# Making the second half's matmul operands in four parts instead of six, in the later half of a block

## The chip, the cores and the metric

The kernel runs on one core of one Trainium2 chip. The metric is the device time of one execution in microseconds (us). Several engines work side by side on a core, each with its own queue of instructions in a fixed order: PE (TensorE, the matmuls), DVE (VectorE), ACT (ScalarE), POOL (GpSimd) and SP (SyncE, which here issues nearly all transfers). An instruction waits at the head of its queue until what it needs is there, and everything behind it in that queue waits with it.

## The reference

One encoder layer over 2048 tokens of width 1024, all in fp32. Cut to the places that matter here:

```
h = rms_norm(x, norm1_g);  proj = h @ w_in                    # 1024 x 3584
dq, dk, dv, rq, rk, rv, rg = split(proj)                      # seven blocks of 512 columns
a = diff_attention(rms_norm(dq), rms_norm(dk), dv)            # 4 heads, softmax
y = retention(rq, rk, rv) in both directions, gated by rg
x1 = x + concat(a, y) @ w_out
out = x1 + gelu_mlp(rms_norm(x1, norm2_g), w_mlp1, w_mlp2)    # 1024 x 4096 x 1024
```

## The kernel before

Every fp32 operand of a large product is split into a high and a low part (`hi`, `lo`, rounded to fp32r), and a product is three matmuls: high by high, high by low, low by high (lines 36 to 38). `split_sbuf` makes the high part on ACT (line 44) and the low part on DVE (line 50).

The products with w_in and w_mlp1 go in halves of 1024 tokens (g = 0 and g = 1) and in blocks of 512 columns, and each block is one Strassen-Winograd step (`winograd_block`): seven products of half-size matrices instead of eight. The token side of the seven products are the *units*, in the order of PE: b11, b21, t2, t1, t3, b22, t4 (`UNITS`), where t1 to t4 are differences of the quarter matrices b11, b12, b21, b22. The weight side are a11, a12, the sums s2, s1, s3, s4 (made by POOL on line 277) and a22; each is split into `wh` and `wl` two products ahead of its use. The raw weights of a block come in two transfers into tiles r0 and r1 (line 687). They share the tag "raw", with three buffers, with a third tile, x2, so a new x2 can be loaded only when the last reader of the x2 before is done.

The units of the first half are made before its products start. Those of the second half are made beside the first half's products, 128 tokens of each quarter at a time, by the generator `fill_parts`, in blocks 1 to 4 of the w_in stage (rk, rv, rg and q; the seven blocks go rq, rk, rv, rg, q, k, v) and in blocks 1 to 4 of the stage of w_mlp1. For a fill, SP loads x2 (256 tokens; lines 875 and 1489). In the w_in stage the tokens are then normed: ACT sums the squares (L775), DVE and ACT make the root (L68 to L73), DVE scales x2 (L880). Then PE transposes 16 tiles of 128x128 into PSUM (L180, tile `htp`), DVE multiplies them by the gain back into x2 (L183), DVE and POOL make the differences t1 to t4 in place (L146; t1 and t2 on DVE, t3 and t4 on POOL), ACT and DVE split each unit, and SP stores the parts to DRAM (L253: `b11hd`, `b11ld` and so on), from where the second half loads them.

`winograd_block` calls `between(unit)` each time the instructions of a product have been written, and that call draws the next part from the generator; after the block a loop draws what is left. The code is not a fixed schedule: a list scheduler reorders the instructions of each engine by its own estimate, so the place of a part in the code bounds where its instructions go but does not fix it.

In the q block each finished result is also normed per head (L710 and L711 for the squares and their sum, L68 to L73 the root, L715 the scaling), transposed on PE (L752, tile `pq`) and split (L59). In the rg block POOL gates the results (L733, L734).

Of the kernel before, what the change touches and what calls it, by code (L numbers as in the profile page):

```python
# [40 lines left out]
def split_sbuf(nc, hi, lo, src, eng_hi, eng_lo):  # L41

    if eng_hi == "act":
        nc.scalar.activation(hi, src, AF.Copy)  # L44
    elif eng_hi == "pool":
        nc.gpsimd.tensor_scalar(hi, src, 1.0, 1.0, op0=ALU.mult, op1=ALU.mult)
    else:
        nc.vector.tensor_copy(hi, src)
    e = nc.gpsimd if eng_lo == "pool" else nc.vector
    e.tensor_tensor(out=lo, in0=src, in1=hi.bitcast(F32), op=ALU.subtract)  # L50
# [36 lines left out]
UNITS = ("b11", "b21", "t2", "t1", "t3", "b22", "t4")  # L87
# [47 lines left out]
def fill_parts(nc, pp, x2, turn, sink):  # L135


    b = {f"b{kh + 1}{th + 1}": x2[:, th, kh * H : (kh + 1) * H] for kh in range(2) for th in range(2)}

    def bring(kh):  # L140
        for th in range(2):
            ps = pp.tile([P, H], F32, tag="p", name="htp")
            turn(ps, kh, th)(b[f"b{kh + 1}{th + 1}"])

    def sub(n, x0, x1, o, eng):
        eng.tensor_tensor(out=b[o], in0=b[x0], in1=b[x1], op=ALU.subtract)  # L146
        b[n] = b[o]

    def split(n):
        hi, lo, then = sink(n)  # L150
        split_sbuf(nc, hi, lo, b[n].rearrange("p (a b) -> p a b", a=4), "act", "dve")
        then()

    bring(0)
    split("b11")
    yield
    bring(1)
    sub("t1", "b12", "b11", "b11", nc.vector)
    split("b21")
    yield  # L160
    sub("t3", "b22", "b12", "b12", nc.gpsimd)
    split("b22")
    split("t1")
    yield
    sub("t2", "b22", "t1", "b22", nc.vector)
    split("t3")
    yield
    sub("t4", "t2", "b21", "b21", nc.gpsimd)
    split("t2")
    yield  # L170
    split("t4")


# [14 lines left out]
class FirstUnits:  # L188
# [7 lines left out]
    def turn(self, kp, kh, th):  # L196
        k = kh * 4 + kp
        ps = self.pp.tile([P, H], F32, tag="p", name="htp")
        for j in range(4):
            self.nc.tensor.transpose(ps[:, j * P : (j + 1) * P], self.xs[th * 4 + j][:, k * P : (k + 1) * P], self.ident[:])  # L200
        self.turned[kp, kh, th] = ps

    def bring(self, kp, kh, th):
        k = kh * 4 + kp
        if (kh, th) == (0, 1):
            t = self.pool2.tile([P, H], F32, tag="hi", name="usrc")
        else:
            t = self.pool.tile([P, H], F32, tag="c", name="usrc", bufs=BUFS["c"])
        ps = self.turned.pop((kp, kh, th))
        self.nc.scalar.activation(t[:], ps[:], AF.Copy, scale=self.gain[:, k : k + 1])  # L210
        self.b[kp][f"b{kh + 1}{th + 1}"] = t[:]

    def split(self, kp, n, hi, lo="dve"):
        split_sbuf(self.nc, *(t[:, kp] for t in self.tb[n]), self.b[kp][n], hi, lo)

    def sub(self, kp, n, x0, x1, o, eng):
        b = self.b[kp]
        eng.tensor_tensor(out=o, in0=b[x0], in1=b[x1], op=ALU.subtract)
        b[n] = o
# [131 lines left out]
class Units:  # L351
# [13 lines left out]
    def next(self, shape, dt, name):  # L365
        self.n += 1
        return self.shared.tile(shape, dt, tag=f"p{(self.n - 1) % 6}", name=name, bufs=1)
# [196 lines left out]
def pool(tc, name, bufs, space=None, side=None):  # L564
    kw = {} if space is None else dict(space=space)
    return tc.tile_pool(name=name, bufs=bufs, side=side, reuse_waits="tile", **kw)
# [3 lines left out]
def encoder(ctx: ExitStack, tc: tile.TileContext, a: dict, out: bass.AP, dbg=None):  # L570
    nc = tc.nc
# [10 lines left out]
    def const(shape, name, dt=F32, pool=cp):  # L582
        return pool.tile(shape, dt, tag=name, name=name)
# [41 lines left out]
    t0, t1, t2 = (const([P, 24], f"lgt{i}") for i in range(3))  # L625
# [64 lines left out]
    def load_w(pool, w, c0):  # L690

        return [r for fh in range(2) for r in load_half(pool, w, c0 + fh * 256)]
# [5 lines left out]
    pp = mixer.enter_context(pool(tc, "ps_1", 8, PSUM))  # L698
    ret = Retention(nc, hp, pp, ident, wk, dict(rk=rk_d, rv=rv_d, rq=rq_d))
    with ExitStack() as ph:  # L700
        wp = ph.enter_context(pool(tc, "wst", 3))
# [94 lines left out]
        tb = winograd_units(nc, hp)  # L796
# [116 lines left out]
        for g in range(S // G):  # L913
            if g:
                first = load_w(wp, w_in, blocks[0][1] * 512)
                tb = winograd_units(nc, hp, saved[0])
            for bi, (what, blk) in enumerate(blocks):
                raws = first if bi == 0 else load_w(wp, w_in, blk * 512)
                if g == 0 and 0 < bi < 5:
                    x2 = second_load(bi - 1)  # L920
                fill = iter(())
                if g == 0 and 0 < bi < 5:
                    fill = fill_parts(
                        nc, pp, x2, turn_pair(nc, (x2[:, 0], x2[:, 1]), g1, ident), into_dram(nc, tp, "hi", saved[0], bi - 1)
                    )

                def between(unit):
                    if g and what == "v":
                        lead_in(unit)
                    if unit != "b11":  # L930
                        next(fill, None)

                winograd_block(nc, wp, pp, raws, tb, what not in ("rq", "rk"), consumer(what, g), later, between,
                    ahead, parts() if g == 0 and bi == 0 else iter(()),
                    dict(s1=s1[:], s2=s2[:]) if g == 0 and bi == 0 else {})
                ahead = {}
                if g == 0 and bi == 0:
                    small_ones()
                for _ in fill:
                    pass  # L940
# [478 lines left out]
    wp = mlp.enter_context(pool(tc, "m1w", 3))  # L1419
    pp = mlp.enter_context(pool(tc, "ps_m1", 8, PSUM))  # L1420

    def load_w1(blk):
        return [r for fh in range(2) for r in load_half(ep, w1, fh * (DFF // 2) + blk * 256)]

    with ExitStack() as ph:
        hp = ph.enter_context(pool(tc, "h2T", 1))
        for g in range(S // G):
# [4 lines left out]
            tb = tb0 | winograd_units(nc, hp, saved[1 + g], UNITS[2:], loads, ("t4", "b22", "t3", "t2", "t1"))  # L1432
            for blk in range(DFF // 512):
# [13 lines left out]
                if blk == 0:  # L1447
                    raws = first
                elif blk == 1:
                    with tc.issue_after(loads[-1].ins):  # L1450
                        raws = load_w1(blk)
                else:
                    raws = load_w1(blk)
# [30 lines left out]
                fill = iter(())  # L1484
                if g == 0 and 0 < blk < 5:
                    x2 = ep.tile([P, 2, DM], F32, tag="raw", name="x2")
                    for i in range(2):
                        r0 = (7 + 4 * i + blk) * P
                        nc.sync.dma_start(x2[:, i], x1n_d[r0 : r0 + P, :])
                    fill = fill_parts(  # L1490
                        nc, pp, x2, turn_pair(nc, (x2[:, 0], x2[:, 1]), g2, ident), into_dram(nc, wp, "d", saved[2], blk - 1)
                    )
                winograd_block(
                    nc, wp, pp, raws, tb, False, consume, [[], []], lambda unit: unit != "b11" and next(fill, None),
                    ahead=ahead, sums=sums, ptag="d",
                )
                ahead = {}
# [144 lines left out]
```

## Time and profile before

| | |
|---|---|
| median of 3 runs | 2854.14 us (2851.39 to 2856.62) |
| profiled execution | 2851.18 us, of which the span 2849.4 us |
| PE busy | 2723.1 us, 96% of the span |
| DVE, POOL, ACT busy | 1917.1, 1346.1 and 1298.5 us |
| stage of w_in, first half | up to about 330 us in the span |
| stage of w_out | 1365 to 1591 us |
| blocks 1 to 4 of w_mlp1, first half | about 1630 to 1800 us |

The span runs from the first to the last instruction that the profiler recorded; 1.8 us of the profiled execution lie around it. PE is the engine that sets the end: it is idle for 126 us of the span (2849.4 less 2723.1), and what counts for the time is where it waits and where its matmuls run at less than the full clock. "Granted clock" is the share of TensorE's full clock that the profile shows for a stretch.

### The profile page before, as it was taken

How to read it: one execution, taken by the hardware profiler on the slowest of the kernel's cores; microseconds unless marked ns; L12 is line 12 of the kernel's file. 1: busy time of each engine (PE TensorE's matmuls, PEld its weight loads, DVE VectorE, ACT ScalarE, POOL GpSimd, SP SyncE). 2: the span in 40 equal slices, each digit the busy share in tenths (PEclk: the TensorE clock that was granted, in tenths of full speed). 3: DMA queues.
4: the chain of work that ended last, by engine and by line, in shares of the span. 5: the costliest groups of instructions: out<-in, count | busy, mean ns of one | idle time of the engine just before them, and what ended most of it. 6: DMA issues, size and time to landing. Idle time of an engine off the chain costs nothing. (4 is left out here: it accounts for less than half of the span.)

```text
span 2849.4 us, 41027 instructions
## 1 busy us (share of the span) xinstructions
PE 2723.1 (96%) x15488; PEld 2333.2 (82%) x15488; DVE 1917.1 (67%) x2877; ACT 1298.5 (46%) x1842; POOL 1346.1 (47%) x778
## 2 busy tenths in 40 slices
PE   5997999998889999999899989999999999999999
PEld 4797989997778888888777777788888888888887
DVE  7888864787788999989887466555655544435432
ACT  5433422344367777777433345444445432222221
POOL 6345222513368777887443355665655103323320
PEclk8998999998899999999999999999999999999999
DMA  3564683269442313121477766767444848755461
GB/s 126 182 205 143 237 283 112 89 194 262 108 107 59 90 52 94 53 87 45 155 238 242 284 199 221 226 237 276 160 159 149 316 156 291 284 200 177 155 243 45
DMA packets 361029, 494.50 MB, mean 174 GB/s; under 512 B 23168, under 2 KB 257152, under 8 KB 352640
## 3 DMA queue, kind: packets, MB, share of 16 engines
q1 hardware_dynamic: 338608, 466.71, 49.9%
q10 hardware_dynamic: 21648, 20.98, 2.2%
q0 software_dynamic: 576, 4.19, 0.4%
q8 instruction: 122, 2.00, 0.3%
q14 instruction: 75, 0.61, 0.1%
HBM read 315.64 MB, written 176.16 MB: 173 GB/s over the span
## 5 line engine op out<-in xcount | busy, mean ns | idle before, releaser
L37 PE MATMUL p<-wl,ah 128*128 128x512 f32 x896 | 348.6, 389 | 0.0
L36 PE MATMUL p<-wh,ah 128*128 128x512 f32 x896 | 348.4, 389 | 0.0
L277 POOL TENSOR_TENSOR s<-raw 128x1024 f32<-128x1024 f32 x58 | 146.2, 2521 | 356.7 <-DMA raw<-in_w_mlp 103.7
L318 DVE TENSOR_TENSOR c<-ps,c 128x512 f32<-128x512 f32 x360 | 237.8, 684 | 114.2 <-PE ps L38 112.3
L1055 POOL TENSOR_TENSOR p<-p 128x1024 f32<-128x1024 f32 x127 | 303.3, 2412 | 0.1
L44 ACT ACTIVATE ah<-ra 128x1024 fp32r<-128x1024 f32 x112 | 112.6, 1052 | 412.5 <-PE p L37 410.8
L50 DVE TENSOR_TENSOR wl<-s,wh 128x1024 fp32r<-128x1024 f32 x120 | 192.1, 1602 | 148.8 <-ACT wh L44 148.7
L1039 ACT ACTIVATE p<-p,nm 128x2048 f32<-128x2048 f32 x128 | 256.8, 2006 | 35.7 <-DVE nm L1027 34.7
L50 DVE TENSOR_TENSOR ah<-ra,ah 128x1024 fp32r<-128x1024 f32 x76 | 103.4, 1396 | 221.4 <-ACT ah L44 221.4
L1465 POOL TENSOR_TENSOR c<-c 128x512 f32<-128x512 f32 x128 | 195.9, 1554 | 105.2 <-ACT c L1468 103.5
L44 ACT ACTIVATE wh<-s 128x1024 fp32r<-128x1024 f32 x120 | 126.5, 1056 | 245.4 <-PE ps L37 104.0
L38 PE MATMUL p<-wh,ah 128*128 128x512 f32 x608 | 236.5, 389 | 0.0
L1526 POOL TENSOR_TENSOR t<-br 128x1024 f32<-128x1024 f32 x32 | 77.7, 2429 | 335.7 <-DMA br<-in_w_mlp 176.4
L1022 PE MATMUL sc<-ka,qa 128*128 128x512 f32 x512 | 207.5, 405 | 4.1 <-DVE nm L1027 3.9
L1054 POOL TENSOR_SCALAR p<-p,ratio 128x1024 f32<-128x1024 f32 x127 | 141.9, 1130 | 144.0 <-DVE ratio L1049 110.8
L1023 PE MATMUL sc<-ka,qb 128*128 128x512 f32 x512 | 202.9, 396 | 0.0
L37 PEld LDWEIGHTS p<-wl,ah 128*128 128x128 f32 x896 | 168.2, 188 | 34.9
L36 PEld LDWEIGHTS p<-wh,ah 128*128 128x128 f32 x896 | 168.2, 188 | 34.9
L55 ACT ACTIVATE aTh<-pa 128x512 fp32r<-128x512 f32 x256 | 151.1, 591 | 83.4 <-PE pa L1216 82.0
L1027 DVE CUSTOM_DVE_ANT_0 p<-sc,bias,nm 128x1024 f32<-128x1024 f32 (+1 forms) x136 | 167.7, 1233 | 22.6 <-PE sc L1023 20.8
L1216 PEld LDWEIGHTS pa<-ident,p 128*128 128x128 f32 x1024 | 120.7, 141 | 64.1 <-issue 30.2
L56 DVE TENSOR_TENSOR aTl<-pa,aTh 128x512 fp32r<-128x512 f32 x256 | 170.3, 686 | 4.0 <-DMA vh<-vhd 3.3
(377 smaller groups left out, 8169.1 us busy)
## 6 DMA issues: line engine op xcount, KB each, us to landing
br<-in_w_mlp SPq DMA_DIRECT2D x88, 512.0 KB, 5.5
raw<-in_w_mlp SPq DMA_DIRECT2D x32, 1024.0 KB, 5.9
raw<-in_w_in SPq DMA_DIRECT2D x28, 1024.0 KB, 5.7
xt<-in_x SPq DMA_DIRECT2D x20, 512.0 KB, 5.5
q<-rqd SPq DMA_DIRECT2D x16, 512.0 KB, 10.2
qa<-qhd SPq DMA_DIRECT2D x64, 128.0 KB, 3.0
qb<-qld SPq DMA_DIRECT2D x64, 128.0 KB, 3.0
ua11d<-c SPq DMA_DIRECT2D x32, 256.0 KB, 2.2
```

The costliest lines, as they stand in the source:

```text
L36: nc.tensor.matmul(out, ah, bh, start=first, stop=False)
L37: nc.tensor.matmul(out, ah, bl, start=False, stop=False)
L38: nc.tensor.matmul(out, al, bh, start=False, stop=last)
L44: nc.scalar.activation(hi, src, AF.Copy)
L50: e.tensor_tensor(out=lo, in0=src, in1=hi.bitcast(F32), op=ALU.subtract)
L56: nc.vector.tensor_tensor(out=lo, in0=src, in1=hi.bitcast(F32), op=ALU.subtract)
L318: nc.vector.tensor_tensor(out=o[:], in0=x0[:], in1=x1[:], op=op)
L1022: nc.tensor.matmul(sc[:, o : o + 512], qa[:, c, ql], r, start=True, stop=False)
L1023: nc.tensor.matmul(sc[:, o : o + 512], qb[:, c, ql], r, start=False, stop=True)
L1039: nc.scalar.activation(p[:], p[:], AF.Exp, bias=nm[:, n : n + 1], scale=-1.0, accum_out=l[:])
L1055: e.tensor_tensor(out=p0, in0=p0, in1=p1, op=ALU.add)
L1465: nc.gpsimd.tensor_tensor(out=u[n][:], in0=u[x0][:], in1=u[x1][:], op=op)
```

## The change

The generator yields four parts instead of six. The transposes of all sixteen tiles now stand together in the first part; the differences t1 and t3 come in the second, t2 and t4 in the third, and the splits are distributed so that the last part holds only t2 and t4. In the w_in stage a part is drawn only behind units with an index over 2 in `UNITS`, that is behind the products t1, t3, b22 and t4; in the stage of w_mlp1 behind those with an index over 1, that is behind t2, t1, t3 and b22. Before, a part was drawn behind each of b21, t2, t1, t3, b22 and t4 in both. The operations themselves, their number, shapes and engines are the same.

```diff
     bring(0)
     split("b11")
+    bring(1)
     yield
-    bring(1)
     sub("t1", "b12", "b11", "b11", nc.vector)
+    sub("t3", "b22", "b12", "b12", nc.gpsimd)
     split("b21")
-    yield
-    sub("t3", "b22", "b12", "b12", nc.gpsimd)
     split("b22")
-    split("t1")
     yield
     sub("t2", "b22", "t1", "b22", nc.vector)
+    sub("t4", "t2", "b21", "b21", nc.gpsimd)
+    split("t1")
     split("t3")
     yield
-    sub("t4", "t2", "b21", "b21", nc.gpsimd)
     split("t2")
-    yield
     split("t4")
...
                 def between(unit):
                     if g and what == "v":
                         lead_in(unit)
-                    if unit != "b11":
+                    if UNITS.index(unit) > 2:
                         next(fill, None)
...
                 winograd_block(
-                    nc, wp, pp, raws, tb, False, consume, [[], []], lambda unit: unit != "b11" and next(fill, None),
+                    nc, wp, pp, raws, tb, False, consume, [[], []], lambda unit: UNITS.index(unit) > 1 and next(fill, None),
                     ahead=ahead, sums=sums, ptag="d",
                 )
```

Three places show how the instructions move. In the changed kernel every line number over 155 is two lower (L1487 there is L1489 here, L275 is L277). On PE the sixteen transposes of a fill stood in two groups of eight, ahead of products t2 and t1; they now stand together, ahead of t3 in the w_in stage and ahead of t1 in the w_mlp1 stage.

SP in block 1 of w_mlp1, the end of a fill; `x<-x1nd` is the load of the next x2, `us` and `ua` are stores of MLP results, `raw` is a load of weights. Before:

```order
L1461 DMA ua22d<-c 128x512
L1461 DMA us1d<-c 128x512
L1461 DMA ua12d<-c 128x512
L1461 DMA us3d<-c 128x512
L1461 DMA ua12d<-c 128x512
L1461 DMA us2d<-c 128x512
L1461 DMA us1d<-c 128x512
L253 DMA t4hd_142<-d_17809 512x1x128
L253 DMA t4ld_143<-d_17810 512x1x128
L1489 DMA x_17833<-x1nd 128x1024 x2
L687 DMA raw<-in_w_mlp 128x8x256
```

And in the changed kernel:

```order
L251 DMA t4hd_142<-d_17757 512x1x128
L251 DMA t2ld_135<-d_17752 512x1x128
L1459 DMA ua22d<-c 128x512
L251 DMA t4ld_143<-d_17758 512x1x128
L1487 DMA x_17833<-x1nd 128x1024 x2
L1459 DMA us1d<-c 128x512
L1459 DMA ua12d<-c 128x512
L1459 DMA us3d<-c 128x512
L1459 DMA ua12d<-c 128x512
L1459 DMA us2d<-c 128x512
L1459 DMA us1d<-c 128x512
```

The load of the next x2 stood behind six stores of results; now it stands ahead of all six.

POOL in the rg block; the first L146 makes t3, the second t4, `s<-raw` is the first weight sum of the next block (it reads r1 of that block), `s<-s,raw` the second. Before:

```order
L277 TENSOR_TENSOR s<-raw 128x1024
L146 TENSOR_TENSOR x_1618<-x_1618 128x512
L733 TENSOR_TENSOR c<-c,sg 128x512 x2
L734 TENSOR_TENSOR c<-c,gng 128x512 x2
L146 TENSOR_TENSOR x_1618<-x_1618 128x512
L733 TENSOR_TENSOR c<-c,sg 128x512
L734 TENSOR_TENSOR c<-c,gng 128x512
L733 TENSOR_TENSOR c<-c,sg 128x512
L734 TENSOR_TENSOR c<-c,gng 128x512
L733 TENSOR_TENSOR c<-c,sg 128x512
L277 TENSOR_TENSOR s<-raw 128x1024
```

And in the changed kernel:

```order
L731 TENSOR_TENSOR c<-c,sg 128x512
L732 TENSOR_TENSOR c<-c,gng 128x512
L731 TENSOR_TENSOR c<-c,sg 128x512
L732 TENSOR_TENSOR c<-c,gng 128x512
L275 TENSOR_TENSOR s<-raw 128x1024
L146 TENSOR_TENSOR x_1618<-x_1618 128x512
L731 TENSOR_TENSOR c<-c,sg 128x512
L275 TENSOR_TENSOR s<-s,raw 128x1024
L731 TENSOR_TENSOR c<-c,sg 128x512
L146 TENSOR_TENSOR x_1618<-x_1618 128x512
```

Both differences stood ahead of the next block's first weight sum; t3 now stands behind the first sum and t4 behind the second.

DVE in the q block, around the head norm of the first results (`st_2387` and `st_2350` are the same statistics in the two programs, `x_2159` is x2). Before:

```order
L183 TENSOR_TENSOR x_2159<-htp,g_153 128x512
L50 TENSOR_TENSOR wl<-s,wh 128x1024
L50 TENSOR_TENSOR hi_2378<-x_2159,hi_2377 128x512
L711 TENSOR_REDUCE st_2387<-sq 128x8
L711 TENSOR_REDUCE st_2403<-sq 128x8
L318 TENSOR_TENSOR c<-ps,c 128x512
L68 TENSOR_SCALAR rsv<-st_2387 128x8
L50 TENSOR_TENSOR hi_2473<-x_2159,hi_2472 128x512
L68 TENSOR_SCALAR rsv<-st_2403 128x8
L318 TENSOR_TENSOR c<-ps,c 128x512
L50 TENSOR_TENSOR hi_2479<-x_2159,hi_2478 128x512
L146 TENSOR_TENSOR x_2159<-x_2159 128x512
```

And in the changed kernel:

```order
L73 SCALAR_TENSOR_TENSOR st_2350<-rst,st_2350 128x8
L316 TENSOR_TENSOR c<-ps,c 128x512
L71 SCALAR_TENSOR_TENSOR rst<-rsv,st_2366 128x8
L713 TENSOR_TENSOR c<-c,st_2350 128x512
L181 TENSOR_TENSOR x_2159<-htp,g_153 128x512
L72 TENSOR_TENSOR rst<-rst,st_2366 128x8
L181 TENSOR_TENSOR x_2159<-htp,g_153 128x512
L50 TENSOR_TENSOR wl<-raw,wh 128x1024
L181 TENSOR_TENSOR x_2159<-htp,g_153 128x512 x2
L73 SCALAR_TENSOR_TENSOR st_2366<-rst,st_2366 128x8
L50 TENSOR_TENSOR hi_2447<-x_2159,hi_2446 128x512
L316 TENSOR_TENSOR c<-ps,c 128x512 x2
```

The statistics of the head norm started behind the fill's gain and went on between its splits; now the first scaling (L713, L715 before) stands ahead of the fill's first gain.

## Rows read from the trace of the kernel before

**Rows 1.** The page: the span, and each engine's busy time with its share and its number of instructions.
```profile
span 2849.4 us, 41027 instructions
PE 2723.1 (96%) x15488; PEld 2333.2 (82%) x15488; DVE 1917.1 (67%) x2877; ACT 1298.5 (46%) x1842; POOL 1346.1 (47%) x778
```

**Rows 2.** What PE waited for, summed by its line and by what ended the wait (us in total, times, longest). The first two rows are of 130 to 320 us of the span, the next two of 1590 to 1800 us, the last of 1365 to 1591 us.
```profile
PE htp L180 <- DVE x L880: 10.8, 1, 10.8
PE pq L752 <- DVE c L715: 4.8, 2, 2.5
...
PE htp L180 <- DMA x<-x1nd: 14.2, 5, 7.1
PE ps L38 <- DVE wl L50: 2.5, 2, 2.1
...
PE mt L1188 <- POOL mx L1178: 8.6, 5, 3.5
```

**Rows 3.** Busy time of each engine by stretch (us and number of instructions), then the granted clock, the share of the DMA engines and GB/s. The first three are of rg, q and v, the last three of blocks 2 to 4 of w_mlp1, each from the end of a block's b21 product on.
```profile
190.00:226.00 36.00, 36.00 (x303) 36.00 (x302) 26.32 (x26) 15.36 (x22) 29.43 (x17) 1.00 0.62 186
...
238.00:270.00 32.00, 27.20 (x216) 26.79 (x214) 28.75 (x47) 11.87 (x19) 10.93 (x5) 0.93 0.52 149
270.00:320.00 50.00, 50.00 (x405) 50.00 (x404) 47.15 (x100) 22.27 (x37) 11.26 (x5) 0.95 0.57 182
...
1686.60:1725.00 38.40, 31.11 (x137) 25.69 (x137) 23.97 (x30) 15.69 (x24) 15.93 (x10) 0.91 0.80 246
1725.00:1771.00 46.00, 42.67 (x183) 34.81 (x182) 29.06 (x34) 21.21 (x32) 25.81 (x15) 0.93 0.72 229
1771.00:1800.00 29.00, 25.27 (x113) 20.57 (x112) 14.45 (x16) 10.42 (x15) 21.08 (x12) 0.94 0.70 223
```

**Rows 4.** The timeline of PE in blocks 2 and 3 of w_mlp1: start, duration, instruction, and in brackets the idle time before it and what ended it. The first row is the start of b11 of block 2.
```profile
1675.60 0.39 PE L36 MATMUL ps<-b11h,wh 128*128 128x512 f32 x1
...
1681.04 0.39 PE L36 MATMUL ps<-b21h,wh 128*128 128x512 f32 x1
...
1693.77 1.12 PE L180 MATMUL htp<-ident,x 128*128 128x128 f32 x4 [7.13 <-DMA x<-x1nd]
1695.82 0.78 PE L36 MATMUL ps<-t2h,wh 128*128 128x512 f32 x1
...
1702.36 1.03 PE L180 MATMUL htp<-ident,x 128*128 128x128 f32 x8
1703.15 0.48 PE L36 MATMUL ps<-t1h,wh 128*128 128x512 f32 x1
```

**Rows 5.** The timeline of SP's queue in block 2 of w_mlp1 (when it issued each transfer).
```profile
1688.71 0.63 SPq L253 DMA_DIRECT2D t4ld<-d  x1
1689.43 1.13 SPq L1489 DMA_DIRECT2D x<-x1nd  x2
```

**Rows 6.** The timeline of PE in rg (the first row, the start of its t3 product) and in q.
```profile
197.74 0.28 PE L36 MATMUL ps<-wh,t3h 128*128 128x256 f32 x1
...
237.46 1.94 PE L180 MATMUL htp<-ident,x 128*128 128x128 f32 x8 [10.79 <-DVE x L880]
239.05 0.56 PE L36 MATMUL ps<-wh,t2h 128*128 128x256 f32 x1
...
246.29 0.36 PE L36 MATMUL ps<-wh,t1h 128*128 128x256 f32 x1
...
252.13 0.28 PE L36 MATMUL ps<-wh,t3h 128*128 128x256 f32 x1
...
266.28 0.65 PE L752 MATMUL pq<-ident,c 128*128 128x128 f32 x4 [2.48 <-DVE c L715]
...
270.00 0.56 PE L36 MATMUL ps<-wh,t4h 128*128 128x256 f32 x1
...
277.84 0.28 PE L36 MATMUL ps<-wh,b11h 128*128 128x256 f32 x1
```

**Rows 7.** How x2 came to the fills of rv and q, from the timelines of SP's queue and DVE: the issue of the load and the scaling that ends its norm (rv, then q).
```profile
126.56 1.46 SPq L875 DMA_DIRECT2D x<-in_x  x2
...
140.67 1.42 DVE L880 TENSOR_SCALAR x<-x,ss 128x1024 f32<-128x1024 f32 x2
...
219.62 1.07 SPq L875 DMA_DIRECT2D x<-in_x  x2
...
234.45 3.52 DVE L880 TENSOR_SCALAR x<-x,ss 128x1024 f32<-128x1024 f32 x2
```

**Rows 8.** The timelines of PE, SP's queue and POOL: in rv the start of the t3 product, the load of the raw weights that the first weight sum waits for, that sum, and in rg one gating step (L733) and in q one difference (L146).
```profile
155.69 0.28 PE L36 MATMUL ps<-wh,t3h 128*128 128x256 f32 x1
...
160.55 0.58 SPq L687 DMA_DIRECT2D raw<-in_w_in  x1
...
167.36 2.40 POOL L277 TENSOR_TENSOR s<-raw 128x1024 f32<-128x1024 f32 x1 [9.22 <-DMA raw<-in_w_in]
...
210.71 1.75 POOL L733 TENSOR_TENSOR c<-c,sg 128x512 f32<-128x512 f32 x1
...
248.26 2.20 POOL L146 TENSOR_TENSOR x<-x 128x512 f32<-128x512 f32 x1 [11.50 <-DVE x L183]
```

**Rows 9.** The timeline of DVE in q: the same split of a unit with POOL's difference of rows 8 beside it and without.
```profile
249.23 1.78 DVE L50 TENSOR_TENSOR hi<-x,hi 128x512 fp32r<-128x512 f32 x1
...
254.07 0.68 DVE L50 TENSOR_TENSOR hi<-x,hi 128x512 fp32r<-128x512 f32 x1
```

## Prediction

> **What bounds the kernel now.** I read the page first. PE is busy for 2723.1 of 2849.4 us [rows 1], so the end is set by PE, and all that can be won is its 126 us of idle time and the time in which its matmuls run at the lower clock. DVE, the next engine, stands at 67%. So I asked next what PE waits for in the two stretches where the fills stand. In the w_in stage it is one wait of 10.8 us for the scaling of x2 and two waits, 4.8 us together, for the head norm of q; in the w_mlp1 stage it is 14.2 us for the load of x2 and only 2.5 us for a weight [rows 2]. The timeline shows where: each time PE has finished b21, meets the first transposes of a fill, and the x2 that they read is not there [rows 4, 6]. The products behind such a wait are also slow: the granted clock is 0.91 to 0.95 in the stretches with a wait and 1.00 in the stretch of rg without one [rows 3].
>
> Why x2 is late is seen on SP. In block 2 of w_mlp1 SP issued the load at 1689.43, right behind the store of the low part of t4 of the fill before, while b11 had started at 1675.60 and PE wanted the tile at about 1686.6; it landed at 1693.77 [rows 4, 5]. x2 has one buffer in turn, so the next load stands behind the last readers of the old tile, and these are the work on t4. The fill thus uses its tile nearly until the next block's fill wants it. In q the load was issued at 219.62 and its norm ended at 237.97 [rows 7].
>
> **The change part by part: w_mlp1.** Nothing is removed or added: the transposes, differences, splits and stores are the same in number and shape. What moves is when a fill begins (its sixteen transposes stand ahead of t1, not half ahead of t2) and when it ends (its last part is drawn behind b22, not behind t4). The first gives 5.44 us, a product (1681.04 less 1675.60 [rows 4]). The second brings the release forward by a product as well, and on SP the load no longer stands behind six stores of MLP results. Even if only the one product is won at the release, block 2's load is issued at about 1684.0 (1689.43 less 5.44) and lands, by the 4.34 us it took (1693.77 less 1689.43), at about 1688.3; PE wants it at 1675.60 + 3 x 5.44 = 1691.9. That leaves 3.6 us of slack in the worst of the three blocks. So I take the whole 14.2 us as gone. The slow clock goes with them. In block 2 the first group of transposes took 1.89 us (1693.77 to 1695.82, less a second wait of 0.16) against 0.79 for the next group, and t2 6.54 against 5.44 [rows 4]: 2.2 us. For blocks 3 and 4 I take the share not granted times the stretch, 0.07 x 46.0 and 0.06 x 29.0 [rows 3], 3.2 and 1.7 us; some of that lies in idle time, so it is an upper end. Sum 7.1, and for this stage 21.3 us, bounds 14.2 and 21.3.
>
> **w_in, the wait for x2 in q.** Here the fill begins two products later, ahead of t3: 5.84 us each (246.29 to 252.13 [rows 6]), 11.7 us, against a wait of 10.79. Were x2 ready when it is now, the wait would be gone with 0.9 us to spare. But it will be ready later, since POOL's t3 now stands behind the next block's first weight sum and t4 behind the second. I count from T, the end of the t1 product. In rv the raw load for that sum was issued 4.9 us behind T and the sum began at T + 11.7 (160.55 and 167.36, T being 155.69 [rows 8]). In rg, from T + 11.7: sum 2.4, t3 2.2, a gating step 1.75, second sum 2.4, another step 1.75, t4 2.2 [rows 8] make T + 24.4; the low split (0.68 to 1.78 us [rows 9]) and the issue of the stores bring the load to about T + 26. In the trace of before it was T + 21.9 (219.62 less 197.74). From the issue to the end of the scaling it took 15.5 us in rv and 18.35 in q [rows 7], so x2 is ready at T + 41.5 to T + 44.4. PE wants it at T + 1.6 (this block's own transposes, 2 x 0.79) + 7 x 5.84 (t3, b22, t4, b11, b21, t2, t1) = T + 42.5. That is between 1 us early and 1.9 us late; I take 2 us of wait, which leaves 8.8 us won, with bounds from 4.8 (x2 four us later still) to 10.8. In rk and rv no gating stands on POOL and x2 comes some 6 us earlier, so no wait arises there. The clock behind the wait: transposes 1.59 against 0.79 and t2 with its transposes 7.24 against 5.84 + 0.79 [rows 4, 6], 1.4 us.
>
> **w_in, the head norm in q.** DVE made the norm's statistics between the gain and the splits of the fill that had come 10.8 us late, and PE waited 2.48 us and then 2.33 for it [rows 2, 6]; t4 behind these took 7.84 us instead of 5.84 [rows 6], so 6.8 us in all. Now the first scaling stands ahead of the fill's gain. But DVE was busy for 28.75 of 32.0 us in q and for 47.15 of 50.0 in v [rows 3], and it will have the same work in some 15 us less. So I take 5 of the 6.8, bounds 0 and 6.8.
>
> **What may be lost.** The work of a fill, spread over six products, now lies in four. PE's short waits for a weight split (2.5 us in all [rows 2], 1.2 us each) show what it costs when DVE or ACT comes late. I charge 0.4 us for each of eight fills, 3 us, bounds 0 and 16 (1.2 us, and a clock loss of the same order in some). In the w_out stage the scheduler also exchanges some rows on SP, DVE and POOL; PE's largest wait there is 8.6 us in five pieces [rows 2], and some pieces grow and others shrink: I take nothing, with 5 us on either side.
>
> **The sum.** 21.3 + 8.8 + 1.4 + 5.0 - 3.0 = 33.5 us. The profiled execution took 2851.18 us, of which 1.8 lie outside the span, and the three runs have a median of 2854.14, so it lies 3.0 us under the median and near the fastest. 2851.2 - 33.5 = 2817.7; I forecast 2818 us.
>
> **The rivals.** First, x2 is late again in q: if POOL's queue in rg puts t4 back by another 8 us (it was busy for 29.43 of the 36 us ahead of the wait [rows 3]), the 10.8 and the clock return, the head norm's wait with them, and only w_mlp1 is won: 2851.2 - 21.3 + 3 = 2833 us.
>
> Second, the bunched fills make DVE late for weights in all blocks: 16 us in place of 3, 2831 us. For it speaks that a split beside one of POOL's differences took 1.78 us instead of 0.68 [rows 9], 1.1 more; the sixteen differences of POOL would lengthen DVE's queue by up to 16 x 1.1 = 17.6 us if each met a split. Against it, DVE has a quarter of its time free in rg (26.32 of 36.0 [rows 3]). The Trainium skill bears on this: its page GPSIMD Engine Reference, section Specifications, says that GpSimd's interfaces to SBUF are shared with VectorE and that they contend when the VectorE instruction has two SBUF inputs, which the split has. By that rule t3 and t4, now drawn in the same parts as more splits, slow DVE; the trace agrees that they can, by the 1.1 us above, but six parts had such pairs too.
>
> Third, slower than before. The difference t2 on DVE is written over b22, which t3 on POOL reads, so t2 waits for t3, and t3 now stands behind the weight sum, and so behind the raw load. DVE's queue behind t2 holds the next block's weight split and the additions that free PSUM. If the raw load lands 5 us later than in rv, PE stands for that long in each fill: eight fills x 5 us = 40 us against a gain of 36.5 without the charge, 2855 us; it decides from 4.6 us in each fill. A wait of that kind isn't seen in the fills of before, and the weights behind t2 have about a product of lead.
>
> Fourth, the change doesn't do what it does on paper in w_mlp1: x2's load, though first on SP, waits for a late t4 of POOL, and half of the 21.3 us stays: 2828 us.
>
> **How the numbers follow.** The forecast has a chance of 0.62, x2 late again in q 0.13, bunched weights 0.12, slower or no change by the stall behind t2 0.08, half of w_mlp1 0.05. The upper side with all bounds at their best is 2851.2 - (21.3 + 10.8 + 1.4 + 6.8 + 5) = 2806. The range goes from 2805 to 2836, which leaves out the third rival and a little beside it. A change of under 0.2% (5.7 us) is about what a measurement of this kernel can't tell from none. By the cases: faster 0.92, within 0.2% 0.04, slower 0.04.
>
> **What would show it right or wrong.** In the profile after, PE should show no wait for the load of x2 in w_mlp1, with a granted clock of 0.99 or more there, and L1487's issue ahead of the MLP stores. In q a wait of 0 to 4 us for L878 should stand ahead of t3, and the head norm's wait should be under 2 us. Waits for a weight (L50, L44) in the fills should sum to under 5 us. The forecast is wrong if x2 in q is more than 6 us late, if PE waits for `wl` in every fill, or if the stretch of w_out, which the change doesn't touch, moves by more than 5 us.

## The result, and the profile after

The changed kernel takes 2833.26 us (median of 4 runs, 2830.59 to 2834.85) against 2855.38 us before on the same chips; the ratio is 0.9923, with a 95% interval of 0.9906 to 0.994. So it is 22 us faster, where 36 had been forecast from the median of before (33.5 from its profiled execution). The profiled execution's span went from 2849.4 to 2831.3 us, 18.1 less. The kernel before, run beside each of the experiments below, had medians from 2855.79 to 2857.38 us. One execution, the fourth of e10, took 4458.21 us; e10's time is the median of its other three.

The page after, the span and the engines' busy time:

```profile
span 2831.3 us, 41049 instructions
PE 2716.9 (96%) x15488; PEld 2332.9 (82%) x15488; DVE 1914.4 (68%) x2877; ACT 1297.6 (46%) x1842; POOL 1350.9 (48%) x778
```

Over the whole span PE does the same 15488 matmuls in 6.2 us less busy time and waits 11.9 us less. Both kernels run the same number of matmuls, so the start of the same matmul can be compared along the span. In the w_in stage the changed kernel falls 11.0 us behind, which the start of the second half's first product shows, in the kernel before and in the changed one:

```profile
364.56 0.40 PE L36 MATMUL ps<-b11h,wh 128*128 128x512 f32 x1
```
```profile
375.53 0.40 PE L36 MATMUL ps<-b11h,wh 128*128 128x512 f32 x1
```

By the end of attention it is 12.9 behind, at the end of w_out 4.0, and behind w_mlp1's four fills it is 18.05 ahead and stays so. By stage that is +11.0, +2.0, -9.0 and -22.0 us. The forecast had -13.7 (15.2 won, less half of the charge of 3), 0, 0 and -19.8.

What PE waited for after, in 130 to 345 us (the first stretch of [rows 2] ends at 320; up to 345 the kernel before has the same two rows), in 1590 to 1800, and in 1365 to 1591 (its largest five).

```profile
PE pq L750 <- DVE c L713: 13.1, 2, 8.6
PE ps L37 <- DVE wl L50: 5.7, 3, 2.4
PE htp L178 <- DVE x L878: 2.3, 1, 2.3
...
PE ps L38 <- DVE wl L50: 2.1, 1, 2.1
PE ps L36 <- ACT wh L44: 1.9, 2, 1.3
...
PE mt L1186 <- POOL mx L1177: 2.8, 4, 0.9
PE mm L36 <- ACT wo L44: 2.3, 1, 2.3
PE mm L38 <- DVE mTb L56: 2.3, 1, 2.3
PE mt L1186 <- POOL mx L1176: 2.0, 2, 1.3
PE mt L1186 <- POOL early L1176: 1.2, 1, 1.2
...
```

In w_mlp1 the 14.2 us for x2 are gone and next to nothing came in their place: the waits for weights sum to 4.0 us, and to 3.5 before. In w_in the wait for x2 shrank from 10.8 to 2.3 us, but the head norm's wait grew from 4.8 to 13.1 and a new wait for weights takes 5.7.

The granted clock by stretch after: q and k, then blocks 2 and 3 of w_mlp1 (to be read against [rows 3]).

```profile
250.00:270.00 20.00, 19.62 (x157) 19.21 (x156) 19.77 (x35) 7.48 (x12) 3.17 (x2) 0.93 0.40 119
270.00:320.00 50.00, 36.82 (x274) 36.26 (x273) 44.28 (x90) 21.30 (x37) 20.40 (x8) 0.83 0.60 186
...
1695.00:1737.00 42.00, 42.00 (x202) 35.19 (x201) 28.52 (x37) 22.93 (x33) 28.11 (x16) 1.00 0.82 259
1737.00:1777.00 40.00, 40.00 (x188) 33.39 (x187) 26.00 (x36) 21.71 (x33) 27.42 (x15) 1.00 0.84 268
```

In w_mlp1 PE is busy throughout at the full clock. From 270 to 320 us the clock is 0.83, where it was 0.95 [rows 3], and from 250 to 270 us DVE is busy for 19.77 of 20 us.

The 11.0 us of w_in are lost late in the stage. The t3 product of q still starts within 0.8 us of the time it had before (252.13 in [rows 6]):

```profile
252.88 0.35 PE L36 MATMUL ps<-wh,t3h 128*128 128x256 f32 x1
```

How x2 came to q after, from the timelines of PE (the first transposes of rg's fill, then of q's), POOL (the weight sum ahead of t3, then t4), ACT and DVE (rg's gating and splits of the fill), SP (the end of the stores and the load of x2) and DVE (the norm's scaling):

```profile
199.25 0.38 PE L178 MATMUL htp<-ident,x 128*128 128x128 f32 x2
214.29 2.39 POOL L275 TENSOR_TENSOR s<-raw 128x1024 f32<-128x1024 f32 x1 [7.86 <-DMA raw<-in_w_in]
225.09 1.71 POOL L146 TENSOR_TENSOR x<-x 128x512 f32<-128x512 f32 x1
226.76 0.63 ACT L730 ACTIVATE sg<-c 128x512 f32<-128x512 f32 x1 [4.53 <-DMA t1ld<-hi]
229.18 2.73 DVE L50 TENSOR_TENSOR hi<-x,hi 128x512 fp32r<-128x512 f32 x1 [0.70 <-POOL c L732]
234.73 1.11 DVE L50 TENSOR_TENSOR hi<-x,hi 128x512 fp32r<-128x512 f32 x1 [0.59 <-DMA t2ld<-hi]
235.87 0.51 SPq L251 DMA_DIRECT2D t4ld<-hi  x1
236.47 1.46 SPq L873 DMA_DIRECT2D x<-in_x  x2
248.26 1.42 DVE L878 TENSOR_SCALAR x<-x,ss 128x1024 f32<-128x1024 f32 x2
249.16 1.07 PE L178 MATMUL htp<-ident,x 128*128 128x128 f32 x4 [2.32 <-DVE x L878]
```

The load is issued 37.2 us behind the end of rg's t1 product, where the first row stands (236.47 less 199.25). It was 21.9 before, and 26 had been worked out. The rows in between show why: ACT stands for 4.53 us until the store of t1's low part has landed, and DVE waits for a store and for the gating. The splits, the gating's sigmoid and the head norm's squares all take tiles of one ring, "hi", of four tiles, and a tile comes free only when its store has landed.

### The profile page after: what moved, and what is told of

Read it like the earlier page. It is cut to its first block, busy times and chain, and to the rows that moved or that the text cites. A ratio compares the mean times of both kernels' runs of the same rounds, so it can differ in the third digit from the quotient of the medians.

```text
span 2831.3 us, 41049 instructions
## 1 busy us (share of the span) xinstructions
PE 2716.9 (96%) x15488; PEld 2332.9 (82%) x15488; DVE 1914.4 (68%) x2877; ACT 1297.6 (46%) x1842; POOL 1350.9 (48%) x778
## 4 chain that ended last, share of the span: by engine, by line
PE 75%; DVE 7%; DMA 4%; ACT 1%; issue 1%; POOL 1%; SPq 0%; ACTq 0%; DVEq 0%; POOLq 0%
PE ps L38 10%; PE ps L36 10%; PE ps L37 10%; PE p L38 7%; PE p L36 7%; PE p L37 7%; PE pa L1214 4%; PE sc L1020 4%; PE sc L1021 4%; PE po L36 2%; PE po L38 2%; PE po L37 2%; DVE kvs L493 1%; PE mm L38 1%; PE mm L37 1%
## 5 line engine op out<-in xcount | busy, mean ns | idle before, releaser
L275 POOL TENSOR_TENSOR s<-raw 128x1024 f32<-128x1024 f32 x58 | 147.6, 2545 | 402.5 <-DMA raw<-in_w_in 143.0
```

## The experiments

Two theories of the w_in stage were put against each other. Theory D: DVE has no free time in q and k, so work that x2's lateness pushes there is paid in full. Theory R: the ring of four tiles holds up splits that now come closer together. Every run below was compared with the kernel before on the same chip, and its profile has line numbers of its own. Up to the end of w_in e1 below has the same instructions in the same order on every engine as the kernel before, and yet its second half starts 3.35 us later (367.91 against 364.56). So a shift of some 3 us in one stage of one trace can't be told from none.

**e1: only the fills of w_mlp1 changed.** The generator of before, under the name `fill_parts6`, and its rule of drawing are kept in w_in.

```diff
-                    if UNITS.index(unit) > 2:
+                    if unit != "b11":
                         next(fill, None)
...
-                    fill = fill_parts(
+                    fill = fill_parts6(
```

> The fills of w_in as before (six parts, drawn behind each product from b21 on), those of w_mlp1 as changed. Both theories of the w_in stage (D: DVE has no free time in q and k, so what PE no longer waits for x2 it waits for the head norm; R: the ring of four hi tiles holds the bunched splits up) expect the w_in stage of before: the x2 wait of 10.8 us in q and the two head norm waits of 4.8 us again, no weight waits in rg and q. The w_mlp1 stage should gain the 22 us it gained in the changed kernel. If the 9 us gained in w_out belong to the fills of w_in (through the scheduler's estimate), they are missing here and the time is 2833 us (2829 to 2837); if they belong to w_mlp1's, 2824 us.

2834.69 us, ratio 0.9925 (0.991 to 0.9939).

**e2: only the fills of w_in changed**, the mirror of e1.

```diff
-                    nc, wp, pp, raws, tb, False, consume, [[], []], lambda unit: UNITS.index(unit) > 1 and next(fill, None),
+                    nc, wp, pp, raws, tb, False, consume, [[], []], lambda unit: unit != "b11" and next(fill, None),
...
-                    fill = fill_parts(
+                    fill = fill_parts6(
```

> The fills of w_in as changed, those of w_mlp1 as before. The mirror of the run above: w_in 11 us longer than before, retention 2 longer, w_mlp1 with its 14.2 us of waits for x2, so 2859 us with the 9 us of w_out (855 + 11 + 2 - 9 over 2000) and 2868 us without.

2857.78 us, ratio 1.0006 (0.9997 to 1.0015). (The sum in its expectation is 2855 + 11 + 2 - 9.) The waits of PE in w_in of e1 (two rows), then in w_in of e2 and in its w_mlp1:

```profile
PE htp L217 <- DVE x L917: 10.8, 1, 10.8
PE pq L789 <- DVE c L752: 6.6, 2, 4.7
```
```profile
PE pq L789 <- DVE c L752: 13.6, 3, 8.3
PE ps L37 <- DVE wl L50: 7.0, 6, 2.4
...
PE htp L217 <- DMA x<-x1nd: 15.6, 6, 7.1
```

The two halves of the change add up within what the runs can tell: w_mlp1's fills alone are worth 21 us, w_in's cost 2 us or nothing, and the whole change is worth 22. Inside e2 the w_in stage ends 13.2 us later than before and the w_out stage gains 8.4 to its last product. In e1 w_out gains nothing and PE has the order of rows there that it has in the kernel before; in e2 it has that of the changed kernel. So the 9 us of w_out come from the scheduler, whose order of w_out changes with the fills of w_in, though no line of w_out was touched. The later runs agree: with PE's order of before w_out gains 1.7 us (e17), with that of the changed kernel 8.2 (e13, e18) and 8.5 (e15).

**e4: w_in's four parts drawn one product earlier.**

```diff
-                    if UNITS.index(unit) > 2:
+                    if UNITS.index(unit) > 1:
```

> The changed kernel, but in w_in the four parts are drawn one product earlier (behind t2, t1, t3 and b22, as in w_mlp1). Theory D: 5.8 us of the fill's DVE work in q now lie ahead of the second pair of head norms, so the head norm's wait falls from 13.1 us to about 7 and the time to about 2827 us; x2 in q stays within 3 us of its 2.3 us wait, since release and need both move by a product. Theory R: the splits are as dense as before, so the weight waits in rg and q stay at about 5.7 us and the head norm's wait too: 2833 us, within 3.

2826.07 us, ratio 0.9892 (0.9875 to 0.9908), as theory D had it in size but not in its reason. The waits of PE in w_in, SP's load of q's x2 and one square of the head norm on ACT:

```profile
PE pq L750 <- DVE c L713: 10.9, 1, 10.9
PE htp L178 <- DVE x L878: 3.0, 2, 1.9
...
216.25 1.09 SPq L873 DMA_DIRECT2D x<-in_x  x2
...
258.76 0.63 ACT L708 ACTIVATE sq<-c 128x512 f32<-128x512 f32 x1 [4.51 <-DMA t3hd<-hi]
```

The head norm's wait did not fall to 7, but the waits for weights went, and x2's load came 20 us earlier than in the changed kernel, its norm 14.2. The second half starts 14.0 us earlier (361.56 against 375.53), far more than the 6 us that D had worked out; 6.3 of them are lost again in w_out, which gains only 2.7 here, so that the total fits D's size is luck. ACT's square stood 4.51 us for a store of the fill, which speaks for R.

**e10: four late parts only in q, six parts in rk, rv and rg.**

```diff
-                    if UNITS.index(unit) > 2:
+                    if UNITS.index(unit) > (2 if what == "q" else 0):
...
-                    fill = fill_parts(
+                    fill = (fill_parts if what == "q" else fill_parts6)(
```

> The changed kernel, but the fills of rk, rv and rg are the six parts of before; only q's fill is in four late parts. x2 for q is then released as early as before and wanted as late as in the changed kernel, so its wait is 0. Theory R: the weight waits in rg and q (5.7 us and about 3 of clock) vanish as the splits of rv and rg are spread again, and the head norm's wait shrinks with the ring less loaded: about 2818 us. Theory D: the weight waits may vanish, but the head norm's wait stays at 13 us or grows by the 2.3 us that x2 no longer costs: 2822 to 2826 us.

2823.86 us, ratio 0.9889 (0.9872 to 0.9905), inside D's range. PE did not wait for x2 at all, and yet its waits in w_in sum to 14.8 us:

```profile
PE pq L789 <- DVE c L752: 10.9, 3, 4.8
PE ps L37 <- DVE wl L50: 2.4, 1, 2.4
PE ps L36 <- ACT wh L44: 1.5, 1, 1.5
```

x2 was normed when it was in the kernel before (238.02), and the second half starts at 366.80, 2.2 us later than before and 8.7 earlier than in the changed kernel. So taking x2 off PE's way does not shorten q and k; having x2 earlier does.

**e9: the head norm's squares in PSUM**, out of the ring.

```diff
-            sq = tp.tile([P, 512], F32, tag="hi", name="sq")
+            sq = pp.tile([P, 512], F32, tag="p", name="sq")
```

> The changed kernel, but the squares of the head norm (tile sq, L706 to L709) go to a PSUM bank instead of a tile of the ring "hi", which they share with the splits of the fills. DVE's and ACT's instructions stay the same. Theory R (the ring of four tiles holds the work up): the squares no longer wait for a fill's stores to land, so the head norm's wait in q and k falls from 13.1 us to 5 or less and the clock behind it returns; the weight waits of 5.7 us in rg stay, as the gating still uses the ring: 2822 us (2818 to 2827). Theory D (DVE has no free time): the same work in the same time, 2833 us within 3.

2834.45 us, ratio 0.9916 (0.9899 to 0.9932): no gain, as D had it. The waits of PE in w_in, its largest four:

```profile
PE ps L36 <- DVE c L316: 8.7, 2, 4.8
PE ps L37 <- DVE wl L50: 6.7, 4, 2.4
PE ps L36 <- ACT c L321: 3.3, 1, 3.3
PE ps L36 <- DVE st L709: 2.9, 1, 2.9
```

The wait for the head norm is gone, as R had it, and waits for PSUM banks that DVE and ACT had not yet read out took its place. That the squares now take a bank themselves has a part in this; the run can't separate the two.

**e7: q's gain on ACT**, with the scale operand of its activation, in q's fill only.

```diff
...
+                nc.scalar.activation(t[:, i * P : (i + 1) * P], ps[:, i * P : (i + 1) * P], AF.Copy, scale=gain[:, k : k + 1])
...
-                        nc, pp, x2, turn_pair(nc, (x2[:, 0], x2[:, 1]), g1, ident), into_dram(nc, tp, "hi", saved[0], bi - 1)
+                        nc, pp, x2, (turn_pair_act if what == "q" else turn_pair)(nc, (x2[:, 0], x2[:, 1]), g1, ident), into_dram(nc, tp, "hi", saved[0], bi - 1)
```

> The changed kernel, but in q's fill the gain after the transposes is multiplied by ACT (sixteen activations of 128x128 with the gain as scale) instead of DVE (four of 128x512, 0.69 us each). Theory D: DVE is relieved of 2.8 us in q, so the head norm's wait falls by 3 us or more, 2829 us. Theory R: the ring is as before, 2833 us within 3.

2832.11 us, ratio 0.9907 (0.9892 to 0.9922): the time doesn't tell D's 2829 from R's 2833. In the trace the w_in stage ends 2.8 us earlier than in the changed kernel (372.70 against 375.53), just the work taken from DVE, but e1 shows that as much comes about between equal programs.

**e13: the draw of e4 with the squares of e9.** Its edits are those two.

> The parts of w_in drawn one product earlier (behind t2, t1, t3 and b22) and the squares of the head norm in PSUM. With the earlier draw alone the time was 2826 us, and PE waited 10.9 us once for the head norm, whose square on ACT had waited 4.5 us for the store of t3's high part. Theory R: that wait falls to under 3 us and the clock behind it returns: 2815 us (2812 to 2820). Theory D: 2826 us within 3.

2817.60 us, ratio 0.9859 (0.9844 to 0.9874). PE's wait for the head norm of 10.9 us is gone, and 5.6 us for PSUM banks came:

```profile
PE ps L36 <- DVE c L316: 5.6, 2, 4.6
PE htp L178 <- DVE x L878: 3.0, 2, 2.0
...
```

Of the 8.5 us against e4 only 1.1 lie in w_in; 1.6 lie in retention and 5.5 in w_out, where PE has the order of the changed kernel and e4 another. So R's size is met within its range, but not by the mechanism it named. With e16 below it is the fastest version here, by 40 us ahead of the kernel before on its chip and by 16 ahead of the changed one.

**e15: the low parts of t1 to t4 written over x2**, ten tiles of the ring in a fill instead of fourteen.

```diff
-        hi, lo, then = sink(n)
-        split_sbuf(nc, hi, lo, b[n].rearrange("p (a b) -> p a b", a=4), "act", "dve")
+        src = b[n].rearrange("p (a b) -> p a b", a=4)
+        hi, lo, then = sink(n, src.bitcast(F32R) if n[0] == "t" else None)
+        split_sbuf(nc, hi, lo, src, "act", "dve")
...
```

> The changed kernel, but the low parts of t1 to t4 are written over x2 in place (they are split behind all the differences) and stored from there, so a fill takes ten tiles of the ring instead of fourteen, with the same instructions. x2 is held until the last of these stores has landed, 3 us longer. Theory R: the weight waits of 5.7 us in rg and q fall to under 2, the head norm's wait by half, and the wait for x2 in q grows from 2.3 to about 5: 2826 us (2822 to 2831). Theory D: no gain, 2833 us or 3 more.

2829.25 us, ratio 0.9897 (0.9882 to 0.9912), inside R's range near its upper end. x2's load came at 233.60, 2.9 us earlier, though x2 was held longer, and 7.2 us behind the end of t4 (226.43) instead of 9.7; but the sizes are not R's: the waits for weights fell only to 4.3 us and the head norm's to 9.5.

**e19: a ring of three tiles.**

```diff
-BUFS = {"c": 10, "d": 17, "s": 3, "us": 6, "ud": 1, "hl": 4, "hi": 4, "raw": 3}
+BUFS = {"c": 10, "d": 17, "s": 3, "us": 6, "ud": 1, "hl": 4, "hi": 3, "raw": 3}
```

> The changed kernel with a ring "hi" of three tiles instead of four in the w_in stage. In the changed kernel SP issued q's x2 load 9.7 us behind POOL's t4 of rg's fill, since four splits still stood behind it at the ring. Theory R: that stretch grows to 13 us or more, the weight waits in rg and q from 5.7 us to 8 or more, and the w_in stage ends at least 4 us later than in the changed kernel: 2838 us or more. Theory D alone (the stage is as long as DVE's work in q and k): no change, 2833 us within 3.

2842.17 us, ratio 0.9948 (0.9931 to 0.9964): the total is R's, and so is its first sign. From the end of POOL's t4 to the load of x2 it is now 15.0 us, where R had 13 or more:

```profile
221.06 2.27 POOL L146 TENSOR_TENSOR x<-x 128x512 f32<-128x512 f32 x1
...
238.30 1.07 SPq L873 DMA_DIRECT2D x<-in_x  x2
...
PE htp L178 <- DVE x L878: 11.8, 1, 11.8
```

But t4 itself ended 3.5 us earlier than in the changed kernel, so the load came only 1.8 us later. The waits for weights fell to 3.2 instead of growing to 8, and PE's largest wait, the last row above, is one that R had not named. The w_in stage ends 3.6 us later (379.17), where R had 4 or more, and another 4 were lost in retention, so part of the total is not R's.

**e17: q's head norm scaled by POOL.**

```diff
-        def rms64(t):
+        def rms64(t, eng):
...
-            nc.vector.tensor_tensor(out=t3, in0=t3, in1=st8[:].unsqueeze(2).to_broadcast([P, 8, 64]), op=ALU.mult)
+            eng.tensor_tensor(out=t3, in0=t3, in1=st8[:].unsqueeze(2).to_broadcast([P, 8, 64]), op=ALU.mult)
...
+                rms64(t, nc.gpsimd if what == "q" and g == 0 else nc.vector)
```

> The changed kernel, but in q of the first half the eight scalings of the head norm (L713, 0.69 us each on DVE) are done by POOL. Theory D: DVE is relieved of 5.5 us in q and k, and the w_in stage ends 5 us earlier than in the changed kernel, 6 us later than before instead of 11. Theory R: it ends no earlier. The scheduler here orders w_out as in the kernel before, which costs 9 us there, so the time is 2837 us by D and 2842 us by R; the shift at the end of the w_in stage decides.

2834.67 us, ratio 0.992 (0.9905 to 0.9935). The shift that decides: the second half starts at 368.21, 7.3 us earlier than in the changed kernel, clear of the 3 us that equal programs differ by, and the head norm's wait fell to 4.9 us:

```profile
PE pq L750 <- POOL c L713: 4.9, 3, 3.6
```

D had 5.5 us of DVE's work for it. The 7 us lost again lie in w_out, which the scheduler here orders as in the kernel before.

**e16: e13 with the gain of e7.**

> The earlier draw in w_in with the squares in PSUM (2817.6 us) and in addition q's gain on ACT. Theory D: another 2.8 us from DVE, 2815 us (2812 to 2817). Theory R: no change, 2817.6 us within 2.

2816.78 us, ratio 0.986 (0.9846 to 0.9875): no gain over e13 (2817.60) that the runs could tell, and a time that lies in the ranges of both theories. x2 was normed 1.1 us later than in e13 (236.28 against 235.14), and the second half starts at 360.44 in both, so D's 2.8 us are not to be seen here, as R had it.

**e18: w_mlp1's four parts drawn one product earlier.**

```diff
-    lambda unit: UNITS.index(unit) > 1 and next(fill, None),
+    lambda unit: UNITS.index(unit) > 0 and next(fill, None),
```

> The changed kernel, but in w_mlp1 the four parts are drawn one product earlier (behind b21, t2, t1 and t3), so the transposes stand where half of them stood before, ahead of t2, and only the earlier end of the fill is left of the change there. By the prediction's working the earlier release alone, 5.4 us and the place ahead of the MLP stores, covers block 2's 7.1 us of wait, with at most 1.7 us left: 2833 us, within 3. If the later start were what counts, the waits of before would return in part: 2840 us or more.

2840.69 us, ratio 0.9943 (0.9928 to 0.9957): 7 us slower than the changed kernel. That is the time of the rival (2840 or more), but not by the wait for x2. In the trace w_mlp1 gains 15.0 us instead of 22.0. The waits of PE in w_mlp1:

```profile
PE ps L38 <- DVE wl L50: 7.9, 4, 2.7
...
```

No wait for x2 is among them: the earlier release alone does cover it, as the working had it; but the splits then meet the weights' splits on DVE, and PE waits 5.8 us more for `wl`. So the place of the draw matters there for the weights, not for x2.

## Why the prediction was right, and where it was not

The direction and the range held, the size did not: 22 us of gain by the medians, 18.1 by the profiled executions, instead of 33.5. Of the prediction's own signs those for w_mlp1 and for x2 in q came true. Three went the other way: the head norm's wait is 13.1 us instead of under 2, the waits for weights sum to 9.7 us instead of under 5, and w_out moved by 9.0 us, where 5 was to show the forecast wrong. That the total still lies in the range is in part luck: w_out's gain of 9.0 us makes up for most of the 11.0 that w_in lost.

**w_mlp1** was right in its terms: 21.3 us worked out, 22.0 measured (and 22.0 again in each of the ten other runs with these fills), the 14.2 us of waits gone and the clock back at 1.00. The load of x2 was worked out at 1684.0 at the latest for block 2; it was issued at 1676.98, ahead of b11's start at 1679.52. e1 has this gain alone, and e18 shows that the earlier release is what takes the wait away.

**The release of x2 in rg** is the step that failed first: "the low split and the issue of the stores bring the load to about T + 26". The load was issued at T + 37.2. The first weight sum began at T + 15.0 instead of T + 11.7 and t4 ended at T + 27.6 instead of T + 24.4, 3.2 us that were in the bounds. But behind t4 the working put one split and its stores, 1.6 us, and the trace has 9.7 us. Splits of t2 and t4 still stood there, and their ring tiles and the gating's in the same ring came free only as stores landed. The trace of before has such waits of 1.0 and 0.6 us on DVE; the working had no term for them. With a ring of three (e19) the 9.7 us became 15.0, with ten ring tiles in a fill (e15) 7.2. Part of the stretch is DVE's own: the split at 229.18 took 2.73 us beside a weight sum on POOL, where one without POOL took 0.68 [rows 9]. The Trainium skill says in GPSIMD Engine Reference, section Specifications, that the two engines contend for SBUF when VectorE's instruction has two SBUF inputs; the trace agrees, with these 2.73 us, and with a price above the 1.1 us of the second rival. That the wait for x2 was still 2.3 us, where 2 had been worked out, is luck, errors that cancel: the load was 11.2 us late, but from its issue to the end of the scaling it took 13.2 us instead of 15.5 to 18.35, and PE too wanted x2 5.1 us later than T + 42.5, for 3.4 us of new waits for weights and the slower clock behind them.

**The head norm in q** failed next: "I take 5 of the 6.8" us as won; 8.3 more were lost, and more clock. The reason had been named there, that DVE would have the same work in 15 us less, but it was weighed as a small deduction. PE's waits were taken for separate things, each with its own price. The runs show that in q and k one quantity sets the end, when x2 comes to DVE. From the time that x2 is normed to the second half's first product:

| kernel | x2 normed | second half starts | between |
|---|---|---|---|
| before | 237.97 | 364.56 | 126.6 |
| after | 249.68 | 375.53 | 125.9 |
| e1 (fills of before) | 238.01 | 367.91 | 129.9 |
| e4 (drawn a product earlier) | 235.50 | 361.56 | 126.1 |
| e10 (six parts but in q) | 238.02 | 366.80 | 128.8 |
| e2 (only w_in changed) | 249.92 | 377.74 | 127.8 |
| e9 (squares in PSUM) | 249.15 | 377.33 | 128.2 |
| e13 (e4 and e9) | 235.14 | 360.44 | 125.3 |
| e15 (ten ring tiles) | 248.88 | 372.55 | 123.7 |
| e19 (ring of three) | 254.28 | 379.17 | 124.9 |
| e7 (gain on ACT) | 249.73 | 372.70 | 123.0 |
| e17 (head norm's scaling on POOL) | 250.86 | 368.21 | 117.4 |
| e16 (e13 and gain on ACT) | 236.28 | 360.44 | 124.2 |
| e18 (w_in as in the changed kernel) | 249.49 | 375.12 | 125.6 |

Where DVE's work is unchanged the last column stays within 124 to 130 us (before and e1, equal in w_in, differ by 3.3), while x2's time moves by 19 us, however the parts are drawn and whatever PE is said to wait for. Less work on DVE shortens it clearly in e17, by 8.5 us against the changed kernel; e7, by 2.9, and e16 are not clear of the others. In the changed kernel DVE has next to no idle time between these two rows, 0.3 of 44 us:

```profile
249.59 1.22 DVE L50 TENSOR_TENSOR wl<-s,wh 128x1024 fp32r<-128x1024 f32 x1
...
293.94 0.19 DVE L70 RECIPROCAL st<-st 128x8 f32<-128x8 f32 x1
```

In the same 44 us from x2's norm on DVE is idle for 4.3 us in the kernel before and 7.0 in e1, so there it is not quite without a gap. x2 normed 11.7 us later thus gives a stage that ends 11.0 us later than before, and 7.6 later than in e1. The wait of 10.8 us before was not there to be won by wanting x2 later (in e10 it was gone, and the stage ended no earlier than before); what shortened the stage was bringing x2 earlier (e4, e13) or taking work from DVE (e17). That fits theory D. R has its share in why x2 is late (e15's load came 2.9 us earlier with fewer ring tiles), and e19, where a smaller ring lengthened the stretch behind t4 as R had it but brought another wait than R had named, shows that R alone doesn't tell the sizes. That e16 gains nothing over e13 speaks for R and against D, though 2.8 us are within what equal programs differ by: D may hold only while x2 is late. This stays open.

**The new waits** were put at 3 us for all fills. In w_mlp1 they are 4.0 us against 3.5 before, in w_in 5.7 us against none, so the term was too low there. What the second rival feared did come about, but smaller: the 28 splits of 128x512 in w_in's fills took 28.0 us of DVE before and 34.4 after, 6.4 more, where the rival had up to 17.6 over both stages.

**w_out**: taken as nothing with 5 us on either side; it was -9.0, outside. e1 and e2 place it with the fills of w_in and the scheduler's order. The waits for `mx` were 8.6 us in L1178's row of [rows 2] and 1.5 in L1179's:

```profile
PE mt L1188 <- POOL mx L1179: 1.5, 3, 0.6
```

They came to 2.0 and 2.8 in the rows of L1176 and L1177 of the changed kernel. The forecast came near the measured total only since this gain replaced part of the one that did not come. The 2.0 us lost in retention stay unexplained; the runs have between -0.4 (e17) and 6 (e19) there, and 0.6 with the fills of before (e1).

The first rival, x2 late again and only w_mlp1 won, was put at 2833 us, which is the time measured; but its parts are not those that came about, for w_in lost 11 us instead of nothing and w_out gained 9.

## What to carry to other kernels

When a wait names a late tile, look at the engine behind it before costing the wait as won: if that engine has next to no idle time from the tile's arrival on, as DVE here for 44 us, wanting the tile later moves the wait to its next result, and an earlier arrival or less work on that engine helps. When work is drawn closer together, count the buffers it goes through and what shares them: here fourteen tiles went through a ring of four, each held until a store had landed, and the end of a fill came 9.7 us behind its last difference instead of 1.6. And compare where the same instruction starts along the span, stage by stage; here a total that agreed with a rival hid a loss of 11 us and an unrelated gain of 9.

## What the runs showed of the hardware

A short wait in the middle of the products cost more than itself. The charge for new waits had been 0.4 us for a fill. Behind the waits of 2.31 and 2.42 us for weights, in the b21 products of the blocks that follow rv and rg, b21 took longer by more than the wait:

```profile
180.51 0.38 PE L37 MATMUL ps<-wl,b21h 128*128 128x256 f32 x1 [2.31 <-DVE wl L50]
227.94 0.39 PE L37 MATMUL ps<-wl,b21h 128*128 128x256 f32 x1 [2.42 <-DVE wl L50]
```

```profile
177.92:187.74 9.82, 7.51 (x50) 7.31 (x49) 6.07 (x6) 1.58 (x2) 3.85 (x2) 0.83 0.81 222
...
225.24:235.18 9.94, 7.52 (x51) 7.32 (x50) 8.65 (x7) 3.48 (x5) 9.94 (x5) 0.83 0.58 168
```

The second pair of rows has the stretch of each b21 product from start to start: 9.82 and 9.94 us, where a product without a wait takes 5.75. The granted clock is 0.83 in both and 1.00 in the products right behind them (from 187.74 and 235.18, 5.75 us each), so part of each stretch ran at the lower of the two levels. Each of the two waits cost some 4.1 us in all, 1.8 of it beyond the wait itself. A wait of 0.98 us in the b11 product between them (218.25 to 225.24, 6.99 us) left the granted clock at 1.00 and cost 0.26 us beyond itself.
